# Parking gate tiles in DRAM through a state-space scan, with earlier loads of decay rows, in a fused hybrid encoder layer

## The chip, the core and the metric

One core of a Trainium2 chip runs the whole layer as one program. The metric is the device time of one execution in microseconds (us), as the median over several runs. PE is the matrix engine (TensorE), DVE the vector engine, ACT the scalar engine, POOL the GpSimd engine, and SP the engine that here issues nearly all transfers (DMAs). Every engine takes its instructions strictly in the order in which they stand in its queue.

## What is computed

512 tokens of width 1024, float32, one layer. Cut to what matters:

```python
h = rmsnorm(x, pre_mix_norm)
z, xbc, dt_raw, q, k, v, gates = split_cols(h @ w_in, IN_SPLITS)
y_ssd  = ssd_branch(z, xbc, dt_raw, ...)      # 8 groups: conv, silu, two scans of 4 chunks of 128, gated rmsnorm, @ w_ssd_out
y_attn = window_attention(q, k, v, sink, rel_table) @ w_attn_out
g = sigmoid(gates + b_gate); g_ssd, g_attn = g[..., :1024], g[..., 1024:]
x = x + rmsnorm((g_ssd * y_ssd + g_attn * y_attn) @ w_o, post_mix_norm)
f = square(relu(rmsnorm(x, pre_mlp_norm) @ w_mlp_in)) @ w_mlp_out
x = x + rmsnorm(f, post_mlp_norm)
```

## The kernel before

Matmul operands are split into a high and a low part, and each product is three matmuls of 128x512 (`mm3`). Weights are read from DRAM into one of three raw buffers (`wr`), ACT casts the high part (`wh`, L454) and POOL subtracts it for the low part (`wl`, L458). A raw buffer is free for the next load when its `wl` is done.

The program is a list of quanta. A quantum is one block of 128 output columns: 8 k-steps of three matmuls into a PSUM bank `pp`, and then what its `done` function does with the bank. Smaller work is hung on a quantum with `at(q, fn)` and emitted when quantum q comes: the attention of 16 heads, and for each of the 8 state-space groups the steps of `ssd_steps`. The places of these steps are the numbers in `SCAN` (L32) and `LAST`: `prep` at 0, 1.5, 3 and 4.5 for the four chunks, and `load=1` says that a chunk's rows are asked for one unit ahead of its `prep` (a unit is about an eighth of a group's quanta).

The names that matter:

- `rf` and `rb` (L1084): tiles of 128x512 with the cumulative decay of four heads, forward and backward, read from the DRAM tensor `csT` and copied to all 128 partitions. `E` (L1090): the same with exponentials, four or two small transfers from `csE`.
- `prep` makes `m` (L1109 to L1112) from `rf`, `rb` and `cb`; PE multiplies `m` by `x` in `outs`.
- `rms` sends a row of sums of squares through DRAM to get the inverse root for each token on all partitions: `rrow<-rstd` (L1171), `rcol<-rrow` (L1172), a power on POOL (L371), `rrow<-rcol` (L1174), `rstd<-rrow` (L361), four steps each of which needs the one ahead of it. `finish` then makes `yT` with four DVE instructions (L1184) that need `rstd`.
- `gate`: 16 tiles of 128x512 with tanh of the gates (L919). Tiles 8 to 15 (attention) are made while the first three groups run. `attn_out_quantum` multiplies each in place by its block of the attention's output (L926), two per group from group 3 on. `ssd_out_done` adds them to the other branch (L1240) after the scan. So these eight tiles are held from their making to the end of the scan.
- `split_y`, `load_wo` (`or`, L1283), `ssd_out_quanta`: what follows the scan.

All 128x512 tiles come from one pool of 83 slots (`Slots`): `get` takes the slot that has been free longest, `put` gives it back. An instruction that writes a tile waits for all users of the tile that had the slot before. For a load this wait stands on SP, and what is behind it on SP waits too.

The order on each engine is not the order of writing. After all instructions are recorded, `Planner.plan` goes through them with assumed durations, picks for each engine the next one by readiness and due time, and the orders found are made binding (`chain`). For a transfer the planner assumes that it starts 900 ns after its issue, moves 300 bytes a nanosecond one transfer after the other, and lands 2000 ns later.

Of the kernel before, what the change touches and what calls it, by code (L numbers as in the profile page):

```python
# [10 lines left out]
F32 = mybir.dt.float32  # L11
# [17 lines left out]
LO_DOWN = "p", "p", "p", "vp"  # L29
WARM = 20  # L30

SCAN = dict(load=1, weigh=(-2, -0.5), states=(0, 1), prep=(0, 1.5, 3, 4.5), outs=(2.5, 5.5), rms=9, finish=12,  # L32
            x_flip=2, b_flip=2)
LAST = dict(SCAN, prep=(0, 1, 3, 4), outs=(2.5, 5.5), rms=8, finish=10)
HEADS = dict(scores=0, flip=2, values=3.5)
BUCKET_STARTS = (1, 2, 3, 4, 5, 6, 7, 8, 12, 16, 23, 32, 46, 64, 91)


# [35 lines left out]
class Planner:  # L74
# [153 lines left out]
    def deadlines(self):  # L228
# [13 lines left out]
            late[n] = min([late[s] - self.AFTER[self.eng[s]] for s in self.post[n]] + [t + 5000.0]) - c  # L242
        return late

    def plan(self, wait=0.3):
        late = self.deadlines()
        left = [len(p) + len(q) for p, q in zip(self.pre, self.turn)]
        ready = [0.0] * len(self.ins)
        avail = {e: [] for e in self.OVERLAP}
        key = [n if self.eng[n] == "PE" else late[n] for n in range(len(self.ins))]  # L250
        for n, k in enumerate(left):
            if not k:
                avail[self.eng[n]].append(n)
        free = dict.fromkeys(self.OVERLAP, 0.0)
        port = {"DVE": 0.0, "POOL": 0.0}
        queue, kind = 0.0, None
        order, self.when = {e: [] for e in self.OVERLAP}, {}
        for _ in self.ins:
            best = None
            for e, some in avail.items():  # L260
                if some:
                    t = max(free[e], min(ready[n] for n in some))
                    if best is None or t < best[0]:
                        best = t, e
            t, e = best
            some = avail[e]
            if e == "PE":
                n = self.next_matmul(some, ready, t, kind)
            else:
                n = min((n for n in some if ready[n] <= t), key=lambda n: (key[n], n))  # L270
                m = min(some, key=lambda n: (key[n], n))
                if ready[m] <= t + wait * self.cost[n][0]:
                    n = m
            some.remove(n)
            order[e].append(n)
            t = self.when[n] = max(t, ready[n])
            c, locks = self.cost[n]
            end = t + c
            if e == "SP":
                aps = self.operands(self.ins[n].outs)  # L280
                size = 4 * math.prod(d[1] for d in aps[0].ap)
                queue = max(queue, t + 900) + size / 300
                free[e], end = end, queue + 2000
            elif e == "PE":
                end += self.change(kind, self.kind[n])
                kind = self.kind[n]
                free[e], end = end, end + 160
            else:
                if locks:
                    other = "POOL" if e == "DVE" else "DVE"  # L290
                    end += max(0.0, port[other] - t - 145)
                    port[e] = end
                free[e] = end - self.OVERLAP[e]
                end += 2500 if "DMA" in type(self.ins[n]).__name__ else 0
            for s in self.post[n]:
                same = self.eng[s] == e == "PE"
                ready[s] = max(ready[s], free[e] if same else end + self.AFTER[self.eng[s]])
                left[s] -= 1
                if not left[s]:
                    avail[self.eng[s]].append(s)  # L300
            for s in self.next[n]:
                ready[s] = max(ready[s], t)
                left[s] -= 1
                if not left[s]:
                    avail[self.eng[s]].append(s)
        self.length = max(free.values())
        return order
# [10 lines left out]
class Trunk:  # L318
# [596 lines left out]
    def gate_quantum(self, m, dst):  # L915

        def done(ps):
            t = dst[m] = self.slots.get("gate")
            self.nc.scalar.activation(t, ps, AF.Tanh, bias=self.gbias(m), scale=0.5)  # L919

        return self.cm(self.d_w_in, C_GS + m * 128, lambda: self.h, done)

    def attn_out_quantum(self, m):
        def done(ps):
            t = self.gate[8 + m]
            self.nc.vector.scalar_tensor_tensor(t, t, 1.0, ps, op0=ALU.add, op1=ALU.mult)  # L926
            if m == 7:
                for hi, lo in self.at_:
                    self.slots.put(hi, lo)

        return self.cm(self.d_w_attn_out[0], m * 128, lambda: self.at_, done)
# [19 lines left out]
    def ssd_quanta(self, g):  # L951
# [21 lines left out]
        def x_done(i):  # L973
            def done(ps):
# [4 lines left out]
                if i == 1:  # L979
                    self.later(SCAN["x_flip"], x_flip)  # L980
            return done
# [8 lines left out]
        def bc_done(key, blk):  # L990
            def done(ps):
# [4 lines left out]
                if key == "B":  # L996
                    self.later(SCAN["b_flip"], b_flip)
            return done
# [204 lines left out]
    def place_ssd(self, g, q):  # L1203

        def place():
            weigh, states0, states1, load, prep, outs, rms, finish = self.ssd_steps(g)
            o = LAST if g == 7 else SCAN
            self.at(q(o["weigh"][0]), lambda: weigh((0, 3)))
# [369 lines left out]
    def build(self):  # L1578
        self.Q, self.P, self.T, self.bt, self.at_ = {}, {}, {}, {}, []
        self.gate, self.grp, self.yT, self.ys, self.mix, self.wo, self.wo_raw = {}, {}, [], [], [], {}, {}  # L1580
        self.h2t, self.h2, self.acc = [], [], {}
        self.pair, self.ag, self.pieces = [], {}, {}
        self.held = {p: [] for p in range(4)}
        self.f = {(p, k): {} for p in range(4) for k in range(4)}
        n = lambda: len(self.quanta)
        self.at(1, self.bias_rows)
        self.at(4, self.vectors)
        self.at(6, self.scan_constants)
        kv = self.kv_quanta()
        self.add(*[self.v_quantum(t) for t in range(NT)], self.dt_quantum(), *kv)  # L1590
        self.add(self.q_quantum(0), self.q_quantum(1))
        ga = [self.gate_quantum(8 + i, self.gate) for i in range(8)]
        q = [self.q_quantum(i) if i > 1 else None for i in range(8)]
        ao = [self.attn_out_quantum(m) for m in range(8)]
        fill = {-1: [q[2], q[3], ga[0]], 0: [q[4], q[5], ga[1], ga[2]], 1: [q[6], q[7], ga[3], ga[4]], 2: ga[5:]}
        for g in range(-1, 8):
            q0 = n()
            if g < 7:
                x0, x1, B, C, z0, z1 = self.ssd_quanta(g + 1)
                f = deque(fill.get(g) or ao[2 * g - 6:2 * g - 4])  # L1600
                f = [[f.popleft()] if f else [] for _ in range(4)]
                self.add(x0, *f[0], x1, *f[1], B, *f[2], C, *f[3], z0, z1)
                if g < 0:
                    a0 = q0
                if g == 2:
                    for h in range(16):
                        self.place_head(h, a0 + h * (n() - a0 - HEADS["values"] - 0.5) / 15)
            else:
                self.add(*[self.gate_quantum(m, self.gate) for m in range(8)])
            if g >= 0:  # L1610
                m = n() - q0
                self.place_ssd(g, lambda i, q0=q0, m=m: q0 + (min(i, m + 2) if g == 7 else round(i * m / 4) / 2 if 0 <= i <= 8 else m + i - 8 if i > 8 else i))
        c0 = n()
        self.at(c0, lambda: self.split_y(0, 14))
        self.add(*self.ssd_out_quanta())
        for i in range(4):
            self.at(c0 + 1 + i, lambda i=i: self.load_wo(0, 2 * i))
            self.at(c0 + 2 + i, lambda i=i: self.split_wo(0, 2 * i))
            self.at(c0 + 6, lambda i=i: self.load_wo(1, 2 * i))
        self.add(*[self.mix_quantum(t) for t in range(NT)])  # L1620
        self.at(n() - 1, lambda: self.flip_h2(0))
        self.at(n() + 1, lambda: self.flip_h2(1))
        self.add(*self.up_halves(SPL))
        self.add(*[self.up_quantum(i) for i in range(SPL, 8)])
        for part in range(4):
            down = self.down_quanta(part)
            if part == 3:
                self.at(n() + 1, self.reload_x1)
            for i in range(8):
                self.add(*down[i:i + 1], *([self.up_quantum(8 * part + 8 + i)] if part < 3 else []))  # L1630
        self.chunks = [c for q in self.quanta for c in q.chunks]
        self.start()
        self.run_quanta()
# [27 lines left out]
```

## Time and profile before

| | |
|---|---|
| median of 3 runs | 1101.49 us (1099.68 to 1102.04) |
| the profiled execution's own time | 1103.06 us |
| its span, first to last instruction | 1101.3 us |
| mean clock granted to PE | 0.996 of full |

The profile has five parts that are read here. The page gives each engine's busy time. The chain of waits goes back from the last instruction to what released it, step by step. The list of waits sums, for each pair, how long one engine's line waited for another. The timeline gives instructions in order of time (start, duration, engine, line, operation, tile written and tiles read, and in brackets the idle time ahead and what ended it). The windows give busy time, PE's granted clock and the transfers of a stretch. Matmuls are pipelined, so that a matmul of 128x512 shows as about 0.39 us long while the next one starts 0.23 us after it; the share of busy time therefore hides waits shorter than about 0.16 us.

### The profile page before, as it was taken

Reading aid. Unit: us, or ns where it says so; the run is one execution under the profiler, and the core shown is the slowest. Engines: PE = TensorE matmul, PEld = TensorE weight load, DVE = VectorE, ACT = ScalarE, POOL = GpSimd, SP = SyncE. Lnnn points to the kernel's source line nnn. Section 1 sums busy time; section 2 is a strip of 40 time slices with the busy share of each in tenths; the row PEclk is TensorE's granted clock in tenths of the full one; section 3 lists DMA queues with packets and bytes.
Section 4 is the critical chain, followed back from the end, with each engine's and each line's share of the span. In section 5 each row is a group of like instructions: output and inputs, shape, how many; then the busy total and the mean of one; then the engine's idle time right before and its main releaser. Section 6 shows DMA issues by size and latency. Waiting matters only on the chain.

```text
span 1101.3 us, 16821 instructions
## 1 busy us (share of the span) xinstructions
PE 1085.8 (99%) x5647; PEld 909.9 (83%) x5647; DVE 749.4 (68%) x1319; ACT 640.5 (58%) x1387; POOL 769.1 (70%) x960
## 2 busy tenths in 40 slices
PE   9999999999999999999999999999999999999997
PEld 8888888887888888788888788888988888888886
DVE  5777787787688686768788762435753565665787
ACT  6466776677667667676678642324545444444443
POOL 3346566557658799798989976622668978978953
PEclk9999999999999999999999999999999999999999
DMA  7334433533544626354655464444312521621532
GB/s 217 111 94 128 122 89 102 146 89 88 126 122 117 153 80 162 113 138 112 160 134 157 121 196 134 118 131 170 118 39 58 179 73 56 188 71 50 161 107 76
DMA packets 210050, 132.27 MB, mean 120 GB/s; under 512 B 11267, under 2 KB 193011, under 8 KB 209964
## 3 DMA queue, kind: packets, MB, share of 16 engines
q1 hardware_dynamic: 209804, 131.14, 42.9%
q8 instruction: 44, 0.72, 0.3%
q14 instruction: 42, 0.34, 0.1%
q10 hardware_dynamic: 160, 0.07, 0.0%
HBM read 126.65 MB, written 4.52 MB: 119 GB/s over the span
## 4 chain that ended last, share of the span: by engine, by line
PE 83%; DVE 5%; DMA 4%; ACT 3%; POOL 3%; issue 2%; SPq 0%; POOLq 0%; DVEq 0%; ACTq 0%
PE pp L376 58%; PE ps L376 22%; PE ps L380 3%; DMA rstd<-rrow 2%; POOL wl L458 1%; DMA rf<-csT 1%; DVE u L941 1%; DVE yT L1184 1%; DVE m L1112 1%; DVE B L941 1%; DMA rrow<-rcol 1%; POOL w L1145 0%; ACT n L1109 0%; DVE m L1111 0%; DVE x L1574 0%
## 5 line engine op out<-in xcount | busy, mean ns | idle before, releaser
L458 POOL TENSOR_TENSOR wl<-wr,wh 128x256 fp32r<-128x256 f32 (+1 forms) x500 | 418.8, 866 | 160.7 <-ACT wh L454 153.2
L376 PE MATMUL pp<-h,wh 128*128 128x512 f32 (+1 forms) x1712 | 525.3, 388 | 0.0
L376 PEld LDWEIGHTS pp<-h,wh 128*128 128x128 f32 x1712 | 317.3, 188 | 63.7 <-issue 1.4
L376 PE MATMUL pp<-h,wl 128*128 128x512 f32 (+1 forms) x856 | 332.4, 388 | 0.0
L376 PEld LDWEIGHTS pp<-h,wl 128*128 128x128 f32 x856 | 161.1, 188 | 32.1 <-issue 0.2
L454 ACT CAST wh<-wr 128x1024 fp32r<-128x1024 f32 x131 | 136.3, 1040 | 87.5 <-PE pp L376 75.9
L1494 POOL TENSOR_TENSOR wl<-wd,wh 128x256 fp32r<-128x256 f32 x140 | 115.7, 855 | 33.3 <-ACT wh L1490 25.1
L1490 ACT CAST wh<-wd 128x512 fp32r<-128x512 f32 x80 | 47.2, 619 | 53.0 <-PE pp L376 18.5
L376 PE MATMUL ps<-wh,fh 128*128 128x512 f32 (+1 forms) x196 | 75.5, 385 | 0.5 <-DVE acc L1540 0.5
L376 PE MATMUL ps<-wl,fh 128*128 128x512 f32 (+1 forms) x196 | 75.4, 385 | 0.0
L376 PE MATMUL ps<-wh,fl 128*128 128x512 f32 (+1 forms) x196 | 75.4, 385 | 0.0
L1370 DVE SCALAR_TENSOR_TENSOR pp<-pp,r 128x512 f32<-128x512 f32 (+1 forms) x31 | 17.6, 568 | 71.7 <-ACT r L1367 71.7
L1109 ACT ACTIVATE n<-cb,tables 128x128 f32<-128x128 f32 x128 | 49.5, 391 | 18.3 <-DVE cb L1100 17.5
L1105 ACT ACTIVATE rf<-rf,tables 128x128 f32<-128x128 f32 x128 | 42.4, 392 | 22.5 <-DMA rf<-csT 22.5
L941 DVE SCALAR_TENSOR_TENSOR u<-pp,cv,u 128x510 f32<-128x510 f32 (+1 forms) x64 | 47.6, 743 | 6.6 <-ACT u L937 5.5
L1494 POOL TENSOR_TENSOR wl<-wt,wh 128x256 fp32r<-128x256 f32 x56 | 45.5, 845 | 8.6 <-ACT wh L1490 4.9
L376 PE MATMUL pp<-yh,wl 128*128 128x512 f32 x128 | 49.9, 390 | 0.5 <-POOL wl L458 0.5
L376 PE MATMUL pp<-yl,wh 128*128 128x512 f32 x128 | 49.9, 390 | 0.0
L376 PE MATMUL pp<-yh,wh 128*128 128x512 f32 x128 | 49.6, 389 | 0.0
L1110 ACT ACTIVATE m<-cb,tables 128x128 f32<-128x128 f32 x128 | 49.1, 388 | 0.0
L1103 POOL TENSOR_TENSOR rb<-rb,tables 128x512 f32<-128x512 f32 x32 | 34.4, 1078 | 19.6 <-DMA rb<-csT 11.8
L873 ACT ACTIVATE P<-P,mx 128x384 f32<-128x384 f32 (+1 forms) x64 | 35.2, 552 | 15.6 <-DVE mx L870 15.6
(240 smaller groups left out, 2126.7 us busy)
## 6 DMA issues: line engine op xcount, KB each, us to landing
wr<-in_w_in SPq DMA_DIRECT2D x74, 512.0 KB, 4.1
wr<-in_w_mlp_in SPq DMA_DIRECT2D x32, 512.0 KB, 4.1
wd<-in_w_mlp_out SPq DMA_DIRECT2D x64, 256.0 KB, 5.2
rf<-csT SPq DMA_DIRECT2D x32, 256.0 KB, 4.3
rb<-csT SPq DMA_DIRECT2D x32, 256.0 KB, 4.5
wr<-in_w_ssd_out SPq DMA_DIRECT2D x14, 512.0 KB, 4.2
E<-csE SPq DMA_DIRECT2D x96, 64.0 KB, 3.6
x<-in_x SPq DMA_DIRECT2D x16, 256.0 KB, 5.0
```

The source lines that it names most:

```text
L376: self.nc.tensor.matmul(out, lhsT, rhs, start=start, stop=stop, skip_group_check=more)
L380: self.nc.tensor.transpose(out, src, self.ident[:n, :n])
L454: self.nc.scalar.copy(hi[:, :m], raw)
L458: engines[e].tensor_tensor(lo[:, c], raw[:, c], hi[:, c].bitcast(F32), op=ALU.subtract)
L873: nc.scalar.activation(p[:, :w], p[:, :w], AF.Exp, bias=mx[:, n:n + 1], accum_out=sm[:, n:n + 1])
L941: nc.vector.scalar_tensor_tensor(u[:, a:e], ps[:, a + d:e + d], self.wtap(t, b), u[:, a:e], op0=ALU.mult, op1=ALU.add)
L1103: nc.gpsimd.tensor_tensor(v4(rb), v4(rb), cs[:, 1].unsqueeze(2).to_broadcast([128, 4, 128]), op=ALU.subtract)
L1105: nc.scalar.activation(v4(rf)[:, h], v4(rf)[:, h], AF.Identity, bias=ncs[:, 0, h:h + 1])
L1109: nc.scalar.activation(v4(n)[:, h], cb[:, 0], AF.Copy, scale=dt[:, 0, h:h + 1])
L1110: nc.scalar.activation(v4(m)[:, h], cb[:, 1], AF.Copy, scale=dt[:, 1, h:h + 1])
L1490: nc.scalar.copy(hi, w)
L1494: (nc.vector if e == "v" else nc.gpsimd).tensor_tensor(low[:, q], w[:, q], hi[:, q].bitcast(F32), op=ALU.subtract)
```

## The change

Four things, in one diff:

1. `load=3`: rows `rf`, `rb` and `E` of a chunk are asked for three units ahead of `prep`, not one (in `LAST` too, which copies `SCAN`).
2. Gate tiles 8 to 15 are written to a DRAM tensor `gd` as soon as tanh is done (`spill`), and their slot is given back. Two quanta ahead of `attn_out_quantum(m)` the tile is read back (`fetch`). Its product is spilled again, and fetched two quanta ahead of `ssd_out_done`. That is 16 writes and 16 reads of 256 KB, all issued by SP.
3. The planner's costs of a transfer: it starts 1000 ns after issue, lands 1300 ns after its bytes are through, and bytes a nanosecond depend on the tensor (120 for `csT`, 100 for `csE` and small ones, 270 for weights, 310 otherwise).
4. The planner holds SP back while eight transfers are under way.

No instruction of PE, ACT, DVE or POOL is added or taken away; the order on the engines is planned anew.

```diff
-SCAN = dict(load=1, weigh=(-2, -0.5), states=(0, 1), prep=(0, 1.5, 3, 4.5), outs=(2.5, 5.5), rms=9, finish=12,
+SCAN = dict(load=3, weigh=(-2, -0.5), states=(0, 1), prep=(0, 1.5, 3, 4.5), outs=(2.5, 5.5), rms=9, finish=12,
             x_flip=2, b_flip=2)
+FETCH = 2
...
+    LEAD, TAIL = 1000, 1300
+
+    def transfer(self, n):
+        dst, src = self.operands(self.ins[n].outs)[0], self.operands(self.ins[n].ins)[0]
+        size = 4 * math.prod(d[1] for d in dst.ap)
+        rows = {"csT": 120, "csE": 100, "in_w_in": 270, "in_w_mlp_in": 270, "in_w_ssd_out": 270, "in_w_attn_out": 270}
+        return size / rows.get(src.tensor.name.rsplit("_", 1)[0] if src.tensor.name.startswith("cs") else src.tensor.name, 100 if size < 2 ** 17 else 310)
...
             if e == "SP":
-                aps = self.operands(self.ins[n].outs)
-                size = 4 * math.prod(d[1] for d in aps[0].ap)
-                queue = max(queue, t + 900) + size / 300
-                free[e], end = end, queue + 2000
+                queue = max(queue, t + self.LEAD) + self.transfer(n)
+                free[e], end = end, queue + self.TAIL
+                landed.append(end)
+                if len(landed) >= 8:
+                    free[e] = max(free[e], sorted(landed)[-8])
...
             self.nc.scalar.activation(t, ps, AF.Tanh, bias=self.gbias(m), scale=0.5)
+            if m >= 8:
+                self.spill(m)
...
+    def spill(self, m):
+        t = self.gate.pop(m)
+        self.nc.sync.dma_start(self.gd[(m - 8) * 128:(m - 7) * 128], t)
+        self.slots.put(t)
+
+    def fetch(self, m):
+        t = self.gate[m] = self.slots.get("gate")
+        self.nc.sync.dma_start(t, self.gd[(m - 8) * 128:(m - 7) * 128])
...
             self.nc.vector.scalar_tensor_tensor(t, t, 1.0, ps, op0=ALU.add, op1=ALU.mult)
+            self.spill(8 + m)
...
+        self.gd = self.dp.tile([1024, 512], F32, name="gd")
...
+        for m in range(8):
+            self.at(self.quanta.index(ao[m]) - FETCH, lambda m=m: self.fetch(8 + m))
+            self.at((c0 + 2 if m < 2 else c0 + 1 + m) - FETCH, lambda m=m: self.fetch(8 + m))
```

What the new plan does to the order is shown at three places. Line numbers after the change are 11 to 23 higher (L1084 becomes L1107, L361 L372, L1184 L1207, L1043 L1066). Rows are instructions in the order in which they stand; an "x3" is three of the same kind.

First place: SP in group 1, from the rows of its third chunk to those of its last one. Before (`rf_319` and `rb_320` are the third chunk's, `rf_337` and `rb_338` the last one's, `wr` are weights, `bt` is a head's bias):

```order
L1084 DMA rf_319_2657<-csT_780 128x4x128
L1090 DMA E_321_2661<-csE_781 64x2x128
L1084 DMA rb_320_2658<-csT_780 128x4x128
L1090 DMA E_321_2661<-csE_781 64x2x128 x3
L434 DMA wr_271_2649<-in_w_in 128x8x128
L434 DMA wr_278_2736<-in_w_in 128x8x128
L848 DMA bt_342_2865<-brow_253 128x384
L1084 DMA rb_338_2832<-csT_780 128x4x128
L434 DMA wr_294_2863<-in_w_in 128x8x128
L1084 DMA rf_337_2831<-csT_780 128x4x128
```

After, the same stretch of SP (`rf_315` and `rb_316` are the last chunk's rows, `bt_342`, `wr_271` and `wr_278` the same loads as above):

```order
L1107 DMA rf_315_2614<-csT_781 128x4x128
L1107 DMA rb_316_2615<-csT_781 128x4x128
L1113 DMA E_317_2618<-csE_782 64x2x128
L445 DMA wr_253_2524<-in_w_in 128x8x128
L1113 DMA E_317_2618<-csE_782 64x2x128
L372 DMA rstd_284_2349<-rrow0_2352 128x512
L445 DMA wr_271_2669<-in_w_in 128x8x128
L445 DMA wr_278_2747<-in_w_in 128x8x128
L859 DMA bt_342_2869<-brow_254 128x384
```

The last chunk's rows have moved from behind three weight loads and the bias `bt_342` to ahead of them.

Second place: DVE where group 3 is finished (`yT` from `rstd`) while group 4 is convolved (`u`) and prepared (`rf`, `m`). Before:

```order
L1106 TENSOR_TENSOR rf_624_5438<-rf_624_5438,rb_625_5439 128x512
L941 SCALAR_TENSOR_TENSOR u_591_5133<-pp_511_5079,cv_424,u_591_5133 128x510
L941 SCALAR_TENSOR_TENSOR u_591_5133<-pp_511_5079,cv_424,u_591_5133 128x511 x2
L1184 SCALAR_TENSOR_TENSOR yT_584_5064<-w_468_3990,cv_424,rstd_580_4980 128x256
L1184 SCALAR_TENSOR_TENSOR yT_585_5067<-w_470_4000,cv_424,rstd_580_4980 128x256
L941 SCALAR_TENSOR_TENSOR u_591_5133<-pp_511_5079,cv_424,u_591_5133 128x510
L1106 TENSOR_TENSOR rf_586_5070<-rf_586_5070,rb_587_5071 128x512
L948 SCALAR_TENSOR_TENSOR u_591_5133<-th_592_5139,u_591_5133 128x512
```

After (the first and the last of the four `yT` rows are shown in both):

```order
L964 SCALAR_TENSOR_TENSOR u_598_5160<-pp_511_5106,cv_425,u_598_5160 128x511 x2
L964 SCALAR_TENSOR_TENSOR u_598_5160<-pp_511_5106,cv_425,u_598_5160 128x510
L1135 TENSOR_TENSOR m_601_5182<-m_601_5182,rf_575_4915 128x512
L971 SCALAR_TENSOR_TENSOR u_598_5160<-th_599_5166,u_598_5160 128x512
L1134 TENSOR_TENSOR m_604_5254<-m_604_5254,n_605_5255 128x512
L1135 TENSOR_TENSOR m_604_5254<-m_604_5254,rf_588_5047 128x512
L948 SCALAR_TENSOR_TENSOR gate_586_5003<-gate_586_5003,pp_519_5201 128x512
L1207 SCALAR_TENSOR_TENSOR yT_594_5100<-w_468_3998,cv_425,rstd_587_5008 128x256
L1207 SCALAR_TENSOR_TENSOR yT_595_5103<-w_470_4008,cv_425,rstd_587_5008 128x256
```

`yT` no longer stands in the middle of the convolution of `u` and ahead of `m`, but behind both.

Third place: ACT at the third attention gate in group 0. `xh` is a cast of the scan's weighted input, `th` a tanh for the next convolution, `pT` a copy of attention weights. Before:

```order
L1043 CAST xh_284_2366<-xd_283_2363 128x512
L454 CAST wh_222_2208<-wr_203_2043 128x1024
L919 ACTIVATE gate_260_2206<-pp_221_2181,cv_424 128x512
L947 ACTIVATE th_252_2123<-C_251_2117 128x512
L1005 ACTIVATE th_269_2256<-pp_225_2229 128x512
L890 COPY pT_270_2272<-ps_229_2269 128x256
```

After:

```order
L465 CAST wh_222_2221<-wr_203_2046 128x1024
L930 ACTIVATE gate_263_2218<-pp_221_2193,cv_425 128x512
L970 ACTIVATE th_252_2126<-C_251_2120 128x512
L1066 CAST xh_287_2377<-xd_286_2374 128x512
L1028 ACTIVATE th_275_2276<-pp_225_2242 128x512
L901 COPY pT_276_2292<-ps_229_2289 128x256
```

The cast `xh` has moved behind the gate's tanh: it takes over the gate's slot, and so waits until the gate's spill has landed.

More of the change, by code (lines that the diff above doesn't have):

```diff
@@ L255, in plan @@
         port = {"DVE": 0.0, "POOL": 0.0}
-        queue, kind = 0.0, None
+        queue, kind, landed = 0.0, None, []
         order, self.when = {e: [] for e in self.OVERLAP}, {}
```

## The prediction

> **What bounds the kernel now.** The page first: PE is busy through the whole span, and the chain of waits is mostly PE.
>
> ```profile
> span 1101.3 us, 16821 instructions
> PE 1085.8 (99%) x5647; PEld 909.9 (83%) x5647; DVE 749.4 (68%) x1319; ACT 640.5 (58%) x1387; POOL 769.1 (70%) x960
> ...
> q1 hardware_dynamic: 209804, 131.14, 42.9%
> ...
> PE 83%; DVE 5%; DMA 4%; ACT 3%; POOL 3%; issue 2%; SPq 0%; POOLq 0%; DVEq 0%; ACTq 0%
> ```
>
> Since no matmul is added or taken away, the change can only move the time in which PE waits, and the way its matmuls are interleaved, which the two orders have nearly alike. The chain in order of time tells where that is:
>
> ```profile
> 236.62 7.72 DMA rf<-csT
> ...
> 375.14 7.36 DMA rstd<-rrow
> ...
> 437.55 5.01 DMA rstd<-rrow
> ...
> 632.61 118.93 PE pp L376 x524
> ```
>
> Behind 632 us it is PE after PE (524 matmuls in 118.93 us, 0.227 us each): nothing to win there. Ahead of it the chain leaves PE for transfers, above all of `rf` and `rstd`. The list of waits for PE shows what it lost to others there:
>
> ```profile
> PE ps L376 <- ACT pT L890: 2.3, 3, 1.2
> PE ps L380 <- DVE u L948: 1.4, 1, 1.4
> PE ps L380 <- DVE B L948: 1.1, 2, 0.6
> ...
> PE ps L376 <- DVE m L1112: 0.9, 1, 0.9
> PE ps L376 <- DVE E L1140: 0.6, 1, 0.6
> ...
> PE pp L376 <- POOL wl L458: 0.5, 1, 0.5
> ```
>
> The two rows left out belong to the first and the last instructions, which stay. These six are 6.8 us, all between 40 and 635 us. That is the stake, with one thing more.
>
> **Place one, 254 us.** PE waits twice, and then its clock is halved. Rows of PE's timeline, then windows (us, busy times, PE's granted clock as the number ahead of the last two):
>
> ```profile
> 254.80 0.39 PE L376 MATMUL ps<-KH,Q 128*128 128x256 f32 x1 [1.21 <-ACT pT L890]
> ...
> 256.21 0.44 PE L376 MATMUL ps<-KH,Q 128*128 128x384 f32 x1 [0.56 <-DVE E L1140]
> ...
> 256.00:258.00 2.00, 1.79 (x7) 1.56 (x8) 2.00 (x6) 0.50 (x2) 2.00 (x4) 0.70 0.97 279
> 258.00:260.00 2.00, 2.00 (x7) 1.51 (x6) 1.58 (x7) 0.29 (x1) 1.92 (x4) 0.50 0.70 167
> 260.00:262.00 2.00, 2.00 (x10) 1.66 (x9) 0.00 (x0) 2.00 (x9) 1.92 (x4) 0.95 0.90 198
> ```
>
> The waits are 1.77 us; the clock (0.70, 0.50, 0.95 in three stretches of 2 us) loses 2 x (0.30 + 0.50 + 0.05) = 1.7 us more. Together 3.5 us. The cause is upstream: SP and ACT, same view.
>
> ```profile
> 227.92 0.38 SPq L434 DMA_DIRECT2D wr<-in_w_in  x1
> ...
> 234.17 0.34 SPq L848 DMA_DIRECT2D bt<-brow  x1
> ...
> 236.62 0.36 SPq L1084 DMA_DIRECT2D rf<-csT  x1
> ...
> 244.42 1.28 ACT L1105 ACTIVATE rf<-rf,tables 128x128 f32<-128x128 f32 x4 [2.56 <-DMA rf<-csT]
> ```
>
> SP stood for six microseconds ahead of the bias `bt`, whose slot was not free, and the rows of group 1's last chunk stood behind it. They landed 7.7 us after issue, ACT stood 2.56 us for `rf`, and everything behind `rf` on ACT (`x`, the convolution of `B`, `pT`) came late to PE. In the new order these rows stand three weight loads and that bias earlier. I take the whole 3.5 us as won.
>
> [...]
>
> **Place two, `rstd`.** DVE serves in order, and it stood for a transfer:
>
> ```profile
> DVE yT L1184 <- DMA rstd<-rrow: 20.3, 6, 5.4
> ...
> 382.52 2.31 DVE L1184 SCALAR_TENSOR_TENSOR yT<-w,cv,rstd 128x256 f32<-128x256 f32 x3 [4.00 <-DMA rstd<-rrow]
> ...
> 442.59 3.31 DVE L1184 SCALAR_TENSOR_TENSOR yT<-w,cv,rstd 128x256 f32<-128x256 f32 x4 [3.39 <-DMA rstd<-rrow]
> ...
> 434.92 2.53 SPq L1090 DMA_DIRECT2D E<-csE  x4
> 437.55 0.54 SPq L361 DMA_DIRECT2D rstd<-rrow  x1
> ...
> 395.40 0.66 PE L376 MATMUL ps<-m,x 128*64 128x128 f32 x8 [0.89 <-DVE m L1112]
> ...
> 448.07 0.87 PE L380 MATMUL ps<-ident,u 128*128 128x128 f32 x6 [1.43 <-DVE u L948]
> ...
> 459.67 0.66 PE L380 MATMUL ps<-ident,B 128*128 128x128 f32 x4 [0.51 <-DVE B L948]
> ...
> 513.01 0.66 PE L380 MATMUL ps<-ident,B 128*128 128x128 f32 x4 [0.60 <-DVE B L948]
> ```
>
> `rstd` of group 3 was issued behind four `E` (2.53 us of issuing), DVE stood 3.39 us, and `u` behind it came 1.43 us late to PE. The other three rows have the same history: DVE's list late by `yT`, then `m` or `B` late (at 513 us the rows of `csT` too). Together 0.89 + 1.43 + 0.51 + 0.60 = 3.4 us. In the new order `yT` of group 3 stands behind the rest of `u` and two `m`, so that the same late `rstd` holds up nothing that PE asks for next; groups 2 and 4 read likewise in the two orders. I take 3.4 us as won. Left are `pT` twice (1.1 us) and `wl` (0.5 us), which the moved rows don't explain: 1.6 us, no gain.
>
> **What is added.** 32 transfers of 256 KB. The nearest rows are the same sort later in this kernel: issues by line, KB, median us to landing; then issue times of one of them (ns min, median, max), waits of SP, two rows of ACT's timeline, and the landings of `E`.
>
> ```profile
> E<-csE SPq DMA_DIRECT2D x96, 64.0 KB, 3.6
> ...
> x1d<-x SPq DMA_DIRECT2D x8, 256.0 KB, 2.6
> x<-x1d SPq DMA_DIRECT2D x8, 256.0 KB, 2.7
> ...
> L1334 SPq DMA_DIRECT2D x1d<-x x8: 319/323/339, 733.7 to 768.8; - x8
> ...
> SPq L434 <- POOL wl L458: 295.2, 106, 8.6
> ...
> 187.26 0.68 ACT L919 ACTIVATE gate<-pp,cv 128x512 f32<-128x512 f32 x1
> ...
> 192.00 0.60 ACT L1005 ACTIVATE th<-pp 128x512 f32<-128x512 f32 x1 [3.13 <-PE pp L376]
> ...
> DMA to landing us min/median/max: 2.6/3.6/7.2
> ```
>
> - SP's issuing: 32 x 0.32 = 10 us in some 550 us. SP stands 295 us just for weight buffers; that idle time hides it. Cost 0. Without this cover it would be at most 10 us of lateness, spread over 32 places.
> - The bytes: 32 x 256 KB = 8.4 MB beside 131.14 MB which take 42.9% of the DMA engines: 2.7 points more. Cost 0 as long as no burst meets a due row.
> - The fetches stand two quanta ahead, 2 x 24 x 0.227 = 10.9 us against a landing of 2.7 us. Hidden, cost 0.
> - The spills bring new waits. At the third place of the order ACT's `xh` takes the gate's slot. By the rows: tanh ends at 187.94, issue 0.32 and landing 2.6 make 190.9, the cast (0.60, as `th`) ends at 191.5, and ACT's next one, `th`, was free to start at 192.00 only. So it just fits, with 0.5 us to spare. If the landing takes what the slowest `E` took (7.2), ACT is 4.1 us late there: between 0 and 4.1 us for this place.
> - Rows held two units longer, against eight slots given back one by one while groups -1 to 2 run: in the first half slots are shorter than later. A new order also has misses of its own. The old one had 6.8 us of them in 600 us. The ends are 0 (all as planned) and 6.8 (as many as before); I take a quarter, 1.7 us, since in the later half, where four of the six big waits were, distances grow and slots are plenty.
>
> **Sum.** -3.5 - 3.4 + 1.7 = -5.2 us. The profiled execution took 1103.06 us (span 1101.3 and 1.8 around it), 1.57 above the median, so 1097.9 profiled. That 1.57 is nearly the price of the half clock (1.7): it may be that the median runs don't pay it. Then the median gains 3.5 and comes to 1098.0; if they pay it, 1101.49 - 5.2 = 1096.3. I say 1097.0.
>
> **Rivals.**
> - *The waits move.* Rows asked for earlier hold slots, and what stood behind `rf` stands behind `bt` or a spill now; the misses come back to their old 6.8 us. For: in the first half a load's slot is still taken from something just finished. Against: the long stands for `rstd` had a cause that the order removes. Time: 1101.49 less at most the half clock, 1099.8 to 1101.5.
> - *Slower: a spill holds ACT.* SP reaches the spill late because the weight load two rows ahead of it waits for its buffer (2.8 us in the mean, 295.2/106; 8.6 at worst). ACT stands at `xh`, PE runs dry, and over some 1.8 us of waits the clock is halved for 1.7 us more, as at 256 us. It decides when the new waits exceed 6.9 + 2.2 = 9.1 us: two places, each about 3 us late at PE and with its half clock. Time: about 1104 to 1107. Against: most of the other spilled slots are taken up many rows later.
> - *All misses go.* -3.5 - 3.4 - 1.6 and no new ones: 1101.49 - 8.5 = 1093.0.
> - *The half clock isn't in the timed runs.* Then only waits count: -1.8 - 3.4 + 1.7 = -3.5, 1098.0. For: the 1.57 us between profile and median. [...]
>
> **Numbers.** Forecast near 1097.0, chance 0.46 (its own range 1094.5 to 1099.3); waits only, 1098.0, 0.12; all misses gone, 0.12; waits move, 0.20; slower, 0.10. A change of 0.2% (2.2 us) is about what the measurement tells from none. Faster: 0.46 + 0.12 + 0.12 = 0.70; same 0.20; slower 0.10. The range goes from 1092.5, below the case without misses, to 1102.0, above the case in which the waits move; the slower case stays out.
>
> **What would show it.** Right: no wait of PE near 254 us and full clock in all windows of 200 to 300 us; DVE's wait for `rstd` well below 20.3 us, or as long but with no wait of PE behind it; no long stand of ACT for `rf`; spills landing in 2.6 us. Wrong: PE waiting for `pT` or `m` at new places between 90 and 320 us with ACT's `xh` released by a transfer to `gd`; a half clock anywhere; the total of PE's waits ahead of 635 us still near 6.8 us.

## The result, and the profile after

| | before | after |
|---|---|---|
| median, the 7 runs of each measured together | 1101.22 us (1099.3 to 1102.04) | 1097.11 us (1096.24 to 1098.17) |
| ratio, 95% interval | | 0.9966 [0.9954, 0.9978] |
| the profiled execution | 1103.06 us, span 1101.3 | 1097.11 us, span 1095.3 |

Faster by 4.1 us in the median and by 5.95 us between the two profiled executions; 1097.0 had been forecast. A second measurement on another chip gave the same ratio (1097.17 against 1100.18 us, 0.9966 [0.9952, 0.9979], 9 runs). Two of the 64 runs of before beside the experiments took 1829 us at a granted clock of 0.556 and are left out of all comparisons.

The page of after: PE's busy time falls by 2.0 us, and 8.4 MB are added on SP's queue (131.14 to 139.53 MB, 42.9 to 44.8%).

```profile
span 1095.3 us, 16847 instructions
PE 1083.8 (99%) x5647; PEld 910.1 (83%) x5647; DVE 759.7 (69%) x1319; ACT 640.5 (58%) x1387; POOL 771.3 (70%) x960
...
q1 hardware_dynamic: 214412, 139.53, 44.8%
```

The list of waits for PE in after (us in total, times, longest; the two rows left out belong to the first and the last instructions, as before):

```profile
PE ps L387 <- ACT pT L901: 1.5, 2, 1.1
...
PE pp L387 <- DVE yl L1255: 1.0, 1, 1.0
PE pp L387 <- DVE h L1350: 0.5, 1, 0.5
```

Six rows of 6.8 us have become three of 3.0 us. `u`, `B`, `m`, `E` and `wl` are out of the list, and two of the three waits for `pT` are gone. The third one stayed and grew. It belongs to the same matmul in both orders (PE's timeline, before and then after):

```profile
86.83 0.44 PE L376 MATMUL ps<-KH,Q 128*128 128x384 f32 x1 [0.47 <-ACT pT L890]
```
```profile
88.27 0.44 PE L387 MATMUL ps<-KH,Q 128*128 128x384 f32 x1 [1.13 <-ACT pT L901]
```

The next matmul of the same shape waits 0.39 us more in after. New are the waits at 643 us (`yl`) and 760 us (`h`). At place one, windows of after (PE's granted clock is the number ahead of the last two):

```profile
254.00:256.00 2.00, 2.00 (x13) 1.82 (x13) 1.91 (x7) 1.50 (x2) 0.96 (x2) 1.00 1.04 297
256.00:258.00 2.00, 2.00 (x10) 1.62 (x9) 1.20 (x5) 0.87 (x4) 2.00 (x4) 1.00 0.57 155
258.00:260.00 2.00, 2.00 (x10) 1.68 (x9) 0.21 (x1) 2.00 (x8) 2.00 (x4) 1.00 0.88 285
```

PE is full and its clock is 1.00, where before had 0.70 and 0.50. The two stands upstream, first ACT's row of before (the other one, 20.3 us, stands in the prediction), then the list of waits of after:

```profile
ACT rf L1105 <- DMA rf<-csT: 22.5, 17, 3.2
```
```profile
DVE yT L1207 <- DMA rstd<-rrow: 9.0, 3, 8.6
...
ACT rf L1128 <- DMA rf<-csT: 1.7, 3, 1.0
```

DVE's stands for `rstd` inside the scan have all but gone: five of 15.0 us in total before, two of 0.4 us in after. What is left is one stand behind group 7, longer than before's 5.4 us there, and PE's new wait for `yl` at 643 us comes right behind it:

```profile
639.69 3.45 DVE L1207 SCALAR_TENSOR_TENSOR yT<-w,cv,rstd 128x256 f32<-128x256 f32 x4 [8.64 <-DMA rstd<-rrow]
```

And ACT at the third place of the order, where the cast `xh` takes the slot of a spilled gate:

```profile
189.06 0.68 ACT L930 ACTIVATE gate<-pp,cv 128x512 f32<-128x512 f32 x1
...
192.89 0.62 ACT L1066 CAST xh<-xd 128x512 fp32r<-128x512 f32 x1 [1.38 <-DMA gd<-gate]
193.78 0.60 ACT L1028 ACTIVATE th<-pp 128x512 f32<-128x512 f32 x1 [0.27 <-PE pp L387]
```

The cast waits 1.38 us for the spill to land, and the `th` behind it still waits 0.27 us for PE: the spill costs nothing there.

### The profile page after: what moved, and what is told of

Same layout as the page of the kernel before. It is cut to its first block, busy times and chain, and to the rows that moved or that the text cites. A ratio compares the mean times of both kernels' runs of the same rounds, so it can differ in the third digit from the quotient of the medians.

```text
span 1095.3 us, 16847 instructions
## 1 busy us (share of the span) xinstructions
PE 1083.8 (99%) x5647; PEld 910.1 (83%) x5647; DVE 759.7 (69%) x1319; ACT 640.5 (58%) x1387; POOL 771.3 (70%) x960
## 3 DMA queue, kind: packets, MB, share of 16 engines
q1 hardware_dynamic: 214412, 139.53, 44.8%
## 5 line engine op out<-in xcount | busy, mean ns | idle before, releaser
L469 POOL TENSOR_TENSOR wl<-wr,wh 128x256 fp32r<-128x256 f32 (+1 forms) x500 | 412.1, 853 | 161.0 <-ACT wh L465 151.7
L1168 POOL TENSOR_TENSOR w<-w,E 128x256 f32<-128x256 f32 x48 | 42.1, 891 | 12.3 <-DVE w L1164 5.9
L1062 POOL TENSOR_TENSOR xd<-x,tables 128x256 f32<-128x256 f32 x48 | 35.5, 757 | 17.6 <-ACT x L987 14.7
```

What stands on the lines that cost most here:

```text
L469: engines[e].tensor_tensor(lo[:, c], raw[:, c], hi[:, c].bitcast(F32), op=ALU.subtract)
L1062: nc.gpsimd.tensor_tensor(v4(xd[:, d * 256:(d + 1) * 256]), v4(xs(c)), by_dir(self.coef, c)[:, d].unsqueeze(2).to_broadcast([128, 4, 64]), ...
L1168: nc.gpsimd.tensor_tensor(wc, wc, E[:, d], op=ALU.add)
```

## The experiments

Theories at the start. S: the spills give slots back, so that rows can be asked ahead of the bias `bt`; the planner's costs only put `yT` later. C: the planner's costs are the change. D: any new order has a draw of misses of its own, and the time follows these. There were twelve runs; here is the whole, with PE's waits in the profile (first and last instruction left out) and the windows of half clock between the first microseconds of the span and the last, each 3.41 us long.

| kernel | spills | planner's costs | units ahead | ratio to before, 95% | waits of PE, us | half windows |
|---|---|---|---|---|---|---|
| before (two profiles) | no | old | 1 | 1 | 6.8; 5.0 | 1; 0 |
| e1 | no | new | 1 | 1.0053 [1.0034, 1.0072] | 8.4 | 4 |
| e2 | yes | old | 1 | 0.9968 [0.9959, 0.9977] | 1.3 | 0 |
| e12 | yes | old | 2 | 0.9965 [0.9953, 0.9978] | 2.3 | 0 |
| e3 | yes | old | 3 | 0.9990 [0.9980, 1.0001] | 3.2 | 1 |
| e4 | yes | new | 1 | 1.0000 [0.9991, 1.0010] | 3.5 | 1 |
| after (two profiles) | yes | new | 3 | 0.9966 [0.9952, 0.9979] | 3.0; 2.1 | 0; 0 |
| e7 | yes | new, no limit | 3 | 0.9959 [0.9945, 0.9973] | 2.6 | 0 |
| e10 | yes | new, no limit | 2 | 1.0063 [1.0051, 1.0076] | 9.3 | 2 |
| e11 | yes | new, no limit | 4 | 0.9940 [0.9926, 0.9954] | 1.0 | 0 |
| e5 | first half | old | 1 | 0.9993 [0.9979, 1.0006] | 3.7 | 0 |
| e6 | second half | old | 1 | 0.9988 [0.9977, 0.9999] | 4.2 | 1 |

Take a profiled execution's time, less its waits of PE, less 1.7 us (half of 3.41) for each half window: before 1103.06 - 6.8 - 1.7 = 1094.6, after 1094.1, e1 1110.26 - 8.4 - 6.8 = 1095.1, e11 1093.75 - 1.0 = 1092.8; all fourteen lie between 1092.8 and 1095.7 us, while their times range over 16.5 us. So most of what separates these kernels is waits of PE and half clock; up to 2.9 us between two of them isn't accounted for.

**e1, the costs alone** (from after):

```diff
-SCAN = dict(load=3, ...
+SCAN = dict(load=1, ...
-                self.spill(m)
...
-            self.spill(8 + m)
...
-            self.at(self.quanta.index(ao[m]) - FETCH, lambda m=m: self.fetch(8 + m))
-            self.at((c0 + 2 if m < 2 else c0 + 1 + m) - FETCH, lambda m=m: self.fetch(8 + m))
```

> The planner's new transfer costs and its limit of eight alone: rows asked one unit ahead, no spills. In its order the last chunk's rows of group 1 still stand behind the bias bt, as before; yT of group 3 stands behind u and m, as after. Theory S (the spills give slots back, and that is what lets the rows go ahead of bt; the costs only put yT later): place one stays, with PE waiting about 1.8 us near 255 us and a half clock of some 3.4 us; place two goes; 1101.2 - 3.4 = about 1097.8. Theory C (the costs are the change): both places go, 1097.1. Theory D (any new order is a new draw of misses): waits of PE from 2 to 10 us at places of their own, time anywhere from 1096 to 1104, and the time above after's is the sum of its waits above after's.

Measured: 1105.54 us against 1100.42. Its rows in the list of waits:

```profile
PE pp L387 <- DVE B L961: 2.7, 1, 2.7
PE ps L387 <- ACT pT L901: 2.2, 1, 2.2
PE ps L391 <- DVE P L890: 2.1, 3, 1.4
...
ACT rf L1125 <- DMA rf<-csT: 7.6, 5, 3.3
```

S was wrong on place one: there is no wait near 255 us, although the rows still stand behind `bt`. The timeline shows why. The plan now knows when the rows land, and ACT takes other work first:

```profile
237.31 0.34 SPq L859 DMA_DIRECT2D bt<-brow  x1
...
239.75 0.65 SPq L1104 DMA_DIRECT2D rf<-csT  x1
...
247.68 1.28 ACT L1125 ACTIVATE rf<-rf,tables 128x128 f32<-128x128 f32 x4 [0.32 <-DMA rf<-csT]
```

ACT stands 0.32 us instead of 2.56, and PE asks for what hangs on it at 258.1 us instead of 253.6 (about 3.4 us of this had been lost at 88 us already). C was wrong too: both old places are mended, and the kernel is 0.5% slower, by these three, at 88, 300 and 575 us, each with the clock halved behind it (mean clock 0.992 in this execution, 0.998 in that of after). D's waits at places of their own came true; its upper end, 1104 us, was too low. The profiled execution (1110.26 us) is the slowest of e1's runs, so its waits are probably above the usual ones.

**e2, the spills alone** (from after; without the limit too):

```diff
-SCAN = dict(load=3, ...
+SCAN = dict(load=1, ...
...
-                queue = max(queue, t + self.LEAD) + self.transfer(n)
-                free[e], end = end, queue + self.TAIL
+                queue = max(queue, t + 900) + size / 300
+                free[e], end = end, queue + 2000
```

> The spills and fetches alone: rows asked one unit ahead, the planner's old transfer costs. In its order the last chunk's rows of group 1 stand ahead of bt, and yT of group 3 behind u and m. Theory S: both places go, so nearly the whole gain comes, 1097 to 1098; PE's waits ahead of 635 us about 2 us. Theory C: with the old costs no gain, 1101.2, waits near 6.8 us. Theory D: 1096 to 1104 with waits elsewhere.

Measured: 1096.73 us against 1100.42. Two waits of PE beside the first and the last, and two of the stands upstream:

```profile
PE ps L386 <- DVE pT L900: 0.8, 1, 0.8
...
PE ps L386 <- ACT pT L900: 0.5, 1, 0.5
```
```profile
ACT rf L1127 <- DMA rf<-csT: 22.0, 14, 3.2
...
DVE yT L1206 <- DMA rstd<-rrow: 11.1, 1, 11.1
```

The spills alone bring the whole gain, as S said, and C falls. What is instructive is the stand of ACT for `rf`: 22.0 us, as long as before (22.5), and the kernel is as fast as after, which has 1.7. The length of that stand is set by the planner's costs (15.6 to 25.0 us in the seven profiles with the old ones, 1.7 to 7.6 in the seven with the new), and it does not set the time. What matters is what stands behind it and when PE asks for that.

**e3, after without the new costs; e4, after with one unit.** e3 has e2's lines of `plan` with `load=3`; e4 is one line:

```diff
-SCAN = dict(load=3, ...
+SCAN = dict(load=1, ...
```

> The changed kernel with the planner's old transfer costs and without its limit: spills and rows three units ahead stay. Theory S: 1097.1, as after, within 1 us. Theory C: 1101.2. Theory D: 1096 to 1104. If rows asked earlier than needed cost something that only the right costs avoid, ACT's or DVE's waits for slots (transfers to gd, rf) show it, at 1098 to 1100.

> The changed kernel with the rows asked one unit ahead again: spills, new costs and limit stay. The last chunk's rows of group 1 stand ahead of bt here too, but behind one more weight load than in after. Theory S: 1097.1 within 1 us; the three units give nothing that the slots don't. Rival L (the three units are what makes rf come in time): ACT's waits for rf back near 22 us, PE waiting for pT again near 254 us, 1099 to 1101.

Measured: 1098.95 and 1099.99 us. Theory S expected 1097.1 of both and misses by 1.9 and 2.9 (by 2.3 and 3.3 if after's ratio is taken to the 1100.42 us that before took beside them); neither place of before is back in either. Each has one large wait of its own, e3 for `P` at 151 us, e4 for `pT` at 89 us, and a half window behind it (mean clocks 0.997 and 0.996):

```profile
PE ps L390 <- DVE P L889: 2.1, 2, 1.9
```
```profile
PE ps L387 <- ACT pT L901: 2.2, 1, 2.2
...
ACT rf L1128 <- DMA rf<-csT: 3.7, 3, 2.8
```

Rival L falls with the last row, although its time (1099 to 1101) came true of e4: ACT's stand for `rf` is 3.7 us with one unit, not 22, and there is no wait near 254 us. The range of 1098 to 1100 for e3 came true too, but in the 16 us ahead of its wait neither ACT nor DVE stands for a transfer; DVE stands 2.54 us for ACT there. At the wait of 88 us, which before and after have too, no engine's wait for a transfer stands in the 25 us ahead. DVE is behind all along: its copy of the table `csr` starts at 69.27 us in e4 and 69.69 in after, against 67.15 in before, and in e4 ACT then stands 2.48 us for DVE's `u`. Which entry of the plan puts DVE behind was not tried.

**e5 and e6, half of the spills each** (from e2):

```diff
-            self.spill(8 + m)
...
-            self.at((c0 + 2 if m < 2 else c0 + 1 + m) - FETCH, lambda m=m: self.fetch(8 + m))
```

and for e6

```diff
-            if m >= 8:
-                self.spill(m)
...
-            self.at(self.quanta.index(ao[m]) - FETCH, lambda m=m: self.fetch(8 + m))
```

> Half of the spills alone (old transfer costs, rows one unit ahead): the gate tile is parked from its tanh to attn_out_quantum, and then held, as before the change, to the end of the scan. The eight slots are free while groups 0 to 2 run. The last chunk's rows of group 1 stand ahead of the bias bt in its order; behind group 3 the first yT stands ahead of u's last step, the others behind it. Theory S1 (the slots of the first half are the gain of place one, 3.5 us in the profiled run and about 2 us in runs without the half clock): no wait and no half clock near 254 us; of the gain of 3.7 us of all spills, 2 to 3.5 us: 1097 to 1098.5. Rival S2 (the gain is in the later half): near 1100.4.

> The other half of the spills alone: the gate tile is held from its tanh to attn_out_quantum, as before the change, its product is parked until ssd_out_done. Nothing changes in the first three groups: the rows of group 1's last chunk stand behind bt as before, and PE should wait 1.8 us near 254 us, with the half clock in some runs. Theory S1: place one stays lost, of place two's waits (1.10 at 394, 1.59 at 446, 0.58 at 459, 0.67 at 512 us) some or all go: 1098 to 1099.5. Rival S2: the whole gain, 1096.7.

Measured: 1099.44 and 1099.11 us against 1100.18. The mechanism of S1 shows at place one. Its amount for e5 does not (a gain of 0.7 us, where 2 to 3.5 had been expected); e6 lies in its range. In e5 SP asks for the rows in time and ACT stands 0.53 us; near 254 us there is no wait. But behind 490 us DVE puts `yT` in the middle of `u`, as before had it in group 3, and PE waits for `u` (rows of e5's timeline):

```profile
232.49 0.99 ACT L1126 ACTIVATE rf<-rf,tables 128x128 f32<-128x128 f32 x3 [0.53 <-DMA rf<-csT]
...
491.77 3.20 DVE L1205 SCALAR_TENSOR_TENSOR yT<-w,cv,rstd 128x256 f32<-128x256 f32 x4
...
498.30 0.87 PE L390 MATMUL ps<-ident,u 128*128 128x128 f32 x6 [1.83 <-DVE u L969]
```

In e6 nothing changed ahead of group 3, and place one is there as before (1.21 and 0.56 us of waits there), with its half window at 256.99 us (256.79 before):

```profile
244.38 1.28 ACT L1125 ACTIVATE rf<-rf,tables 128x128 f32<-128x128 f32 x4 [2.48 <-DMA rf<-csT]
...
254.76 0.39 PE L386 MATMUL ps<-KH,Q 128*128 128x256 f32 x1 [1.33 <-ACT pT L900]
...
256.18 0.44 PE L386 MATMUL ps<-KH,Q 128*128 128x384 f32 x1 [0.57 <-DVE E L1160]
```

The waits of 394 to 513 us are gone in e6, and one for `yh` of 1.3 us at 647 us has come. So place one hangs on slots given back in the first half. Place two divides less cleanly: in e5 too the four old waits of 394 to 513 us are gone, and one of the same kind has come, which ends at 498 us. Each half pays for a new miss: 0.7 and 1.1 us remain of 3.7, and the interval of e5 contains 1.

**e7, after without the limit of eight; e8, after again:**

```diff
-                landed.append(end)
-                if len(landed) >= 8:
-                    free[e] = max(free[e], sorted(landed)[-8])
```

> The changed kernel without the planner's limit of eight transfers under way; the rest stays. If the limit matters, SP's rows are planned too early without it and the time rises towards that of the old costs (1099); if it does nothing here, as after within 0.5 us, 1096.4 on this chip. I expect the latter.

> The changed kernel once more, beside the parts of it. By its ratio of 0.9966 to before, 1096.7 where before is 1100.4; a mean clock of 0.998 or 0.999 in nearly all of its runs, since no place of it halves the clock but the first microseconds; and the wait of about 1.8 us near 87 us again.

Measured: 1096.07 and 1097.17 us. The limit has no effect that shows: the intervals overlap by most of their length. After's own second profile has 2.1 us of waits, against 3.0 in the first, and 1.2 us of them near 88 us, where about 1.8 had been expected: the same order loses a different sum in each execution.

**e9, a second profile of before:** no edit.

> The kernel before, a second profile. [...]

Measured: 1099.88 us, mean clock 0.998, and 1.00 from 254 to 262 us. Its waits, and one window:

```profile
PE ps L380 <- DVE u L948: 1.2, 2, 0.7
PE ps L376 <- ACT pT L890: 1.0, 2, 0.6
...
PE ps L380 <- DVE B L948: 0.9, 2, 0.5
PE ps L376 <- DVE m L1112: 0.8, 1, 0.8
PE ps L376 <- DVE E L1140: 0.6, 1, 0.6
...
256.00:258.00 2.00, 2.00 (x11) 1.67 (x10) 2.00 (x8) 0.00 (x0) 1.94 (x3) 1.00 0.79 233
```

The two causes are there again, for 5.0 us in place of 6.8, and without the half clock. So the half clock at 257 us does not come in each execution of before. What brings it this profile does not tell, since the wait for `pT` at 254 us was itself missing here (`E`'s 0.57 us was there).

**e10, e11, e12, the number of units:** `load=2` and `load=4` in e7, `load=2` in e2.

> The changed kernel without the limit of eight, rows asked two units ahead. Theory S (slots matter, the number of units little, and the rest is which misses an order happens to have): 1095.5 to 1099. Rival L (the three units matter with the new costs, as load1 at 1100.0 against 1097.2 suggests): about half way, 1098 to 1099.

> The changed kernel without the limit of eight, rows asked four units ahead. Rival L: as three units or faster, 1095 to 1096.5. Theory S: 1095.5 to 1099 with misses at places of its own; slots held longer show as waits of SP for ACT's or DVE's tiles.

> The spills with the planner's old costs, rows two units ahead (one unit gave 1096.7, three 1099.0). If more units cost slots and so time under the old costs, between the two, 1097.5 to 1098.5. If what lies between those two is only which misses an order happens to have, anywhere from 1096 to 1099.5, with PE's largest wait at a place of its own.

Measured: 1107.62, 1093.75 and 1096.68 us against 1101.09. Two units are slower by 0.63%, three faster by 0.41%, four by 0.60%. S and L both miss e10 and e11. No price of a unit explains the three, nor does e12, which is neither between e2 and e3 nor different from e2. In e10 it is one wait and two half windows behind it (mean clock 0.995; PE's list, then e11's):

```profile
PE ps L384 <- DVE m L1132: 5.9, 1, 5.9
PE ps L384 <- ACT pT L898: 1.5, 1, 1.5
PE pp L384 <- DVE h L1347: 1.1, 1, 1.1
```
```profile
PE pp L384 <- DVE h L1347: 0.8, 1, 0.8
...
PE pp L384 <- ACT yh L1251: 0.2, 1, 0.2
...
DVE yT L1204 <- DMA rstd<-rrow: 11.6, 2, 11.3
```

In e10 PE stands from 565.6 to 571.5 us for `m`: on DVE it comes behind the convolution of `C`, four `yT` and `z`, and ACT makes its parts only from 567 us on. Why the plan puts it so late was not followed further. e11 has nothing left at 88 us nor anywhere in the scan, and DVE still stands 11.3 us once for `rstd`. It is the fastest version: 0.9940 [0.9926, 0.9954], beside 0.9966 [0.9952, 0.9979] for after.

What stands: S for the two places (with the spills both are mended, place one by those of the first half), with the correction of e1 that the costs mend them too, in another way. D for the size: with orders that differ in one number, waits range from 1.0 to 9.3 us. In both pairs that differ in the spills alone, the spilled kernel is faster, by 0.32% (e2 to before) and 0.53% (e4 to e1, from the ratios). Three units ahead without the spills can't be had: with `load=3` alone the pool of 83 slots is empty when a `prep` asks for a tile. Open is what the plan would have to price so that its misses stay away.

## Why the prediction was right, point by point

- **Place one, 3.5 us.** Mechanism right: waits and half clock are gone, and e6, which leaves the first half alone, has both. It is the place in the order that does it. SP still stands 7.8 us there for the slot of a bias in after (5.8 before), but the rows no longer stand behind it. The size was right for the profiled execution, and for the median it lies between 1.8 and 3.5, which the working had left open too: the half clock comes and goes (one half window in the first profile of before, none in e9). Of the 62 runs of before measured beside the experiments 19 have a mean clock of 0.999, too high for a half window (mean 1099.33 us), and 4 have 0.996, too low without one (mean 1102.60); the other 39 can't be told, since the clock is also halved at the end of the span, for 4.8 us in before and 3.9 us in after, where PE has nothing more to do. So the rival "the half clock isn't in the timed runs" holds for a part of the runs; whether it holds for the run that is the median stays open.
- **Place two, 3.4 us.** Right: `m`, `u` and `B` no longer appear in PE's list. As worked out, `yT` of group 3 stands behind `u` and two `m`, with which DVE is done at about 440 us; it comes to `yT` at 440.6 us and finds `rstd` there, so that the stand inside the scan is gone with the waits. The two go together, and these runs don't part them. Behind group 7 they do part: e2 and e11 stand 11.1 and 11.3 us there with 0 and 0.2 us of PE's waits behind it, while after stands 8.6 us and PE then waits 1.0 us for `yl`. The prediction did not single that stand out.
- **Left over, `pT` twice and `wl`, no gain.** Wrong, by 1.1 us: `wl` (0.5 us) and the `pT` at 344 us (0.7 us) went too, since the whole order is new. The `pT` near 87 us (0.5 us) stayed.
- **Costs put at nothing.** SP's issuing, the bytes, the fetches: right for after. The spills land in 2.4 us (2.6 forecast), the fetches in 4.1 (2.7 forecast), far inside two quanta. The one place where a spill holds ACT came out as worked out, at 0 of the 0 to 4.1.
- **New misses, +1.7.** This term was too small: 2.5 us in the first profile, 1.0 of growth at 88 us, 1.0 for `yl` and 0.5 for `h`. They lie ahead of the first spill (104 us) and behind 640 us, and not in the stretch between. Short slots were one of the two reasons given for them, and no run shows that slots brought them.
- **Sum.** For the profiled executions -3.5 - 3.4 - 1.1 + 2.5 = -5.5 (measured -5.95); for the medians -3.8 if the half clock isn't paid there and -5.5 if it is (measured -4.1, nearer the first). The forecast of 1097.0 was met this closely by luck: the 1.1 us that also went and the 0.8 us by which the new misses are larger nearly cancel, and 1097.0 had been put between 1096.3 and 1098.0 without a row that decides.
- **The rivals.** "Waits move" came true in part: 2.5 us of new waits, where it needed nearly all of 6.8. The slower case did not come in after. e1 and e10 have its size, with waits beyond 8 us and the clock halved behind them, but not its cause as far as is shown: e1 has no spills, and e10's wait of 5.9 us is for `m`. "All misses go" is e11 (1.0 us left), at 1093.75 us: 1093.0 had been worked out for it.

## What to carry to other kernels

When orders are planned, price an edit by what the new order loses at PE, wait by wait, and not by the stands it shortens: ACT's 22 us for `rf` cost nothing that shows in e2, and 1.0 to 9.3 us of waits and the half windows behind them made up most of the difference between twelve kernels. A change that moves the order is a draw beside its mechanism, here from 7 us faster (e11) to 7 us slower (e10), so try neighbouring settings (two, three, four units) before keeping or dropping it. And look at several executions before counting a loss in a profile as won.

## What the runs showed of the hardware

In the traces of before and after the granted clock stays for whole multiples of one length. In the profile of before, full clock begins 4.20 us into the span and lasts 252.59 us, the half clock 3.413 us, and full clock again 836.27 us: 74, 1 and 245 times 3.413 us. After has full clock for 1085.44 us, 318 times, beginning 5.95 us into the span. PE's first matmuls of 128x128 show these beginnings too: before starts 7 of them from 3 to 4 us and 10 from 4 to 5 us, after 7 from 5 to 6 us and 11 from 6 to 7 us. In e4 the half clock lasts 3.41 us (90.38 to 93.79), in e1 at 575 us twice that (574.52 to 581.35). In what follows a window is one such length.

What I had not expected is how little idleness the half clock came behind. Windows of before, e4 and after, with PE's busy time as the first number behind the length:

```profile
253.38:256.79 3.41, 1.64 (x12) 1.08 (x9) 2.99 (x6) 2.50 (x5) 3.41 (x5) 1.00 0.33 79
256.79:260.20 3.41, 3.41 (x11) 2.73 (x10) 2.79 (x10) 0.49 (x1) 3.33 (x6) 0.50 0.84 227
```
```profile
86.96:90.38 3.42, 1.44 (x8) 1.22 (x9) 2.50 (x7) 2.62 (x6) 2.79 (x4) 1.00 0.80 222
90.38:93.79 3.41, 3.41 (x10) 2.64 (x9) 1.39 (x7) 1.95 (x7) 0.00 (x0) 0.50 0.62 170
```
```profile
84.46:87.87 3.41, 2.68 (x18) 2.19 (x17) 3.27 (x5) 2.89 (x6) 3.41 (x6) 1.00 0.07 12
87.87:91.29 3.42, 2.62 (x12) 1.99 (x13) 3.33 (x9) 1.63 (x4) 1.73 (x2) 1.00 0.89 240
```

Behind a window in which PE was idle for 1.77 us (before) or 1.98 us (e4) of 3.41 the clock was halved in the next one. In after the waits near 88 us leave PE idle for 0.73 and 0.80 us in two windows, and the clock stays. The eight windows at full clock ahead of a half one had PE busy for 0 us (e10), 1.19, 1.37 and 1.70 (e1), 1.44 (e4), 1.51 (e3), 1.64 (before) and 1.66 (e6). In e3 a single wait of 1.9 us was enough. But in e5 a window at 495 us had 1.58, and no half clock follows. So this busy time, whose ends are modelled, does not part the two; a bound, if there is one, would lie near these two figures, 1.58 and 1.70 us, which is an estimate.

A half window can also be followed by a second one, and with a busier PE than that. In e1 (its window at half clock, the first number behind the length again PE's busy time) and in e10, PE was busy for 2.71 and 1.87 us of the first half window, and the second was at half clock too:

```profile
574.52:577.93 3.41, 2.71 (x7) 2.16 (x8) 3.33 (x5) 0.63 (x1) 3.41 (x5) 0.50 0.00 0
```

In before and e4 PE was busy for all 3.41 us of the half window, and full clock came back. What decides here stays open.
